# Softmax over a 32,768-wide vocabulary: six 32 KB buffers on one DMA queue, and three 64 KB buffers on two

## The chip, the cores and the metric

The kernel runs on one core of a Trainium2 chip. The metric is device time in microseconds (us) of one execution; the kernel before takes 2494.18 us (median of 3 runs, 2492.26 to 2495.42).

## What is computed

A softmax with temperature over the last axis of a float32 array of 16 x 256 x 32,768; the temperature is 1.0.

```python
scaled = logits / temperature
scaled = scaled - scaled.max(axis=-1, keepdims=True)
exp_scaled = np.exp(scaled)
return (exp_scaled / exp_scaled.sum(axis=-1, keepdims=True)).astype(np.float32)
```

536.87 MB are read and as many are written.

## The kernel before

The 4,096 rows are cut into 8,192 half rows of 16,384 numbers (64 KB). A group is 128 half rows, one on each SBUF partition (64 rows in all), so there are G = 64 groups of 8.4 MB. A group is worked on as C = 2 chunks of 8,192 columns (32 KB on each partition, 4.2 MB), and a chunk has one of six buffers (`xs`, the pool of line 47). There are 128 chunks.

`load` (line 58) brings one chunk in as one DMA; in the first and the last group it uses two DMAs of half the size. `exps` (line 94) does for each piece of 8,192 columns (4,096 in the last group) a maximum on VectorE (line 107, stored negated in `nm`) and, in place, an exponential on ScalarE (line 114) which also adds up its results into `ssum`. `factors` (line 123) finds the maximum of the whole row from the pieces: a small reduction, then `combine` (line 81), which swaps neighbouring partitions, since the two halves of a row lie on neighbouring partitions; a tiny exponential `ee` on ScalarE (line 131), the weighted sum on VectorE (line 138), `combine` again, a reciprocal and the factor `f` of each piece (lines 148 to 150). `scales` (line 152) multiplies a piece by its factor: the first half of the columns on VectorE (line 160), the second half on ScalarE (line 163). `store` (line 70) writes a chunk out as one DMA, in the last group as two.

All loads and stores are issued by SyncE (lines 64 and 75), so they stand in one DMA queue, in the order that the list `order` (line 170) gives: six loads, two stores, and then a load and a store by turns. `keep_in_program_order` holds them to it; a load into a buffer waits for the store that frees it. The order of the instructions of VectorE and ScalarE is chosen by the scheduler of the language: in the trace VectorE takes the next chunk's maximum (line 107) while ScalarE is still at the exponential of the chunk before.

```python
order = [("L", i) for i in range(min(_BUFS, n_chunks))] + [("S", 0)]
for i in range(1, n_chunks):
    order.append(("S", i))
    if i + _BUFS - 1 < n_chunks:
        order.append(("L", i + _BUFS - 1))
```

Of the kernel before, what the change touches and what calls it, by code (L numbers as in the profile page):

```python
# [6 lines left out]


_SPLIT = 2
_CW = 8192  # L10
_BUFS = 6
_PIECE = 8192
_LAST_DMA = 4096
_DVE_SHARE = 0.5


@with_exitstack
def kernel(
    ctx: ExitStack,
    tc: tile.TileContext,  # L20
    logits: bass.AP,
    temperature: bass.AP,
    out: bass.AP,
):
    nc = tc.nc
    inv_t = 1.0 / float(temperature)
    P = nc.NUM_PARTITIONS
    fp32 = mybir.dt.float32
    Exp = mybir.ActivationFunctionType.Exp
    Copy = mybir.ActivationFunctionType.Copy  # L30
    X = mybir.AxisListType.X
    A = mybir.AluOpType

    xf = logits.flatten_outer_dims()
    of = out.flatten_outer_dims()
    N, V = xf.shape
    W = V // _SPLIT
    CW = min(_CW, W)
    C = W // CW
    assert W * _SPLIT == V and CW * C == W and (N * _SPLIT) % P == 0  # L40
    x = xf.rearrange("n (h v) -> (n h) v", h=_SPLIT)
    o = of.rearrange("n (h v) -> (n h) v", h=_SPLIT)
    G = N * _SPLIT // P
    n_chunks = G * C
    n_rounds = _SPLIT.bit_length() - 1

    xpool = ctx.enter_context(tc.tile_pool(name="x", bufs=_BUFS))
    spool = ctx.enter_context(tc.tile_pool(name="stats", bufs=3))
    slots = {}
    stats = {}  # L50

    def spans(total: int, step: int) -> list[tuple[int, int]]:
        return [(s, min(step, total - s)) for s in range(0, total, step)]

    def piece(g: int) -> int:
        return _PIECE if g < G - 1 else min(_PIECE, _LAST_DMA)

    def load(i: int) -> None:
        g, c = divmod(i, C)
        xs = xpool.tile([P, CW], fp32, tag="x", name="xs")  # L60
        slots[i] = xs
        for s, n in spans(CW, _LAST_DMA if g in (0, G - 1) else CW):
            tc.keep_in_program_order(
                nc.sync.dma_start(  # L64
                    out=xs[:, s : s + n],
                    in_=x[g * P : (g + 1) * P, c * CW + s : c * CW + s + n],
                )
            )

    def store(i: int) -> None:  # L70
        g, c = divmod(i, C)
        xs = slots.pop(i)
        for s, n in spans(CW, _LAST_DMA if g == G - 1 else CW):
            tc.keep_in_program_order(
                nc.sync.dma_start(  # L75
                    out=o[g * P : (g + 1) * P, c * CW + s : c * CW + s + n],
                    in_=xs[:, s : s + n],
                )
            )

    def combine(v, op) -> None:
        for j in range(n_rounds):
            mask = [i ^ (1 << j) for i in range(32)]
            nc.vector.stream_shuffle(  # L84
                out=v[:, j + 1 : j + 2], in_=v[:, j : j + 1], mask=mask
            )
            nc.vector.tensor_tensor(  # L87
                out=v[:, j + 1 : j + 2],
                in0=v[:, j : j + 1],
                in1=v[:, j + 1 : j + 2],  # L90
                op=op,
            )

    def exps(i: int) -> None:
        g, c = divmod(i, C)
        xs = slots[i]
        ps = spans(CW, piece(g))
        K = C * len(ps)
        if c == 0:
            stats[g] = tuple(  # L100
                spool.tile([P, K], fp32, tag=f"{nm}{K}", name=nm)
                for nm in ("nm", "ssum", "ee", "f", "ttj")
            )
        nm, ssum = stats[g][:2]
        for j, (s, n) in enumerate(ps):
            k = c * len(ps) + j
            nc.vector.tensor_reduce(  # L107
                out=nm[:, k : k + 1], in_=xs[:, s : s + n], axis=X, op=A.max, negate=True
            )
            if inv_t != 1.0:  # L110
                nc.vector.tensor_scalar_mul(
                    out=nm[:, k : k + 1], in0=nm[:, k : k + 1], scalar1=inv_t
                )
            nc.scalar.activation(  # L114
                out=xs[:, s : s + n],
                in_=xs[:, s : s + n],
                func=Exp,
                bias=nm[:, k : k + 1],
                scale=inv_t,
                accum_out=ssum[:, k : k + 1],  # L120
            )

    def factors(g: int) -> None:
        nm, ssum, ee, f, ttj = stats[g]
        nMh = spool.tile([P, 1 + n_rounds], fp32, tag="nMh", name="nMh")
        Sh = spool.tile([P, 1 + n_rounds], fp32, tag="Sh", name="Sh")
        rS = spool.tile([P, 1], fp32, tag="rS", name="rS")
        with tc.high_priority():
            nc.vector.tensor_reduce(out=nMh[:, 0:1], in_=nm, axis=X, op=A.min)  # L129
            combine(nMh, A.min)  # L130
            nc.scalar.activation(  # L131
                out=ee,
                in_=nm,
                func=Exp,
                bias=nMh[:, n_rounds : n_rounds + 1],
                scale=-1.0,
            )
            nc.vector.tensor_tensor_reduce(  # L138
                out=ttj,
                in0=ee,  # L140
                in1=ssum,
                scale=1.0,
                scalar=0.0,
                op0=A.mult,
                op1=A.add,
                accum_out=Sh[:, 0:1],
            )
            combine(Sh, A.add)
            nc.vector.reciprocal(out=rS, in_=Sh[:, n_rounds : n_rounds + 1])  # L149
            nc.vector.tensor_scalar_mul(out=f, in0=ee, scalar1=rS)  # L150

    def scales(i: int) -> None:
        g, c = divmod(i, C)
        xs = slots[i]
        f = stats[g][3]
        ps = spans(CW, piece(g))
        for j, (s, n) in enumerate(ps):
            k = c * len(ps) + j
            cut = int(n * _DVE_SHARE) // 512 * 512
            nc.vector.tensor_scalar_mul(  # L160
                out=xs[:, s : s + cut], in0=xs[:, s : s + cut], scalar1=f[:, k : k + 1]
            )
            nc.scalar.activation(  # L163
                out=xs[:, s + cut : s + n],
                in_=xs[:, s + cut : s + n],
                func=Copy,
                scale=f[:, k : k + 1],
            )

    order = [("L", i) for i in range(min(_BUFS, n_chunks))] + [("S", 0)]  # L170
    for i in range(1, n_chunks):
        order.append(("S", i))
        if i + _BUFS - 1 < n_chunks:
            order.append(("L", i + _BUFS - 1))

    nxt = 0
    done = -1
    loaded = 0
    for kind, i in order:
        if kind == "L":  # L180
            load(i)
            loaded = i + 1
        else:
            g = i // C
            if g > done:
                while nxt < (g + 1) * C:
                    assert nxt < loaded
                    exps(nxt)
                    nxt += 1
                factors(g)  # L190
                done = g
            scales(i)
            store(i)


# [33 lines left out]
```

## Time and profile before

| What | Value |
|---|---|
| Time, median of 3 runs | 2494.18 us |
| Span of the profiled execution | 2493.8 us |
| VectorE (DVE) busy | 1487.4 us |
| ScalarE (ACT) busy | 1405.0 us |
| Mean DMA rate over the span | 431 GB/s |
| Maximum of 128x8192, L107 (VectorE) | 8.68 us each |
| Exponential of 128x8192, L114 (ScalarE) | 7.12 us each |
| Multiplication of 128x4096, L160 (VectorE) / L163 (ScalarE) | 2.35 / 3.70 us each |

The span is counted from the first to the last instruction of the profiled execution. Busy time of an engine counts its compute instructions only; the issuing of DMAs by SyncE (SP) is not among them. A DMA's transfer is done by 16 DMA engines at once: each of them moves its share of the partitions as a row of packets, one packet for each partition's contiguous run of bytes, and then a small packet that signals the semaphore.

### The profile page before, as it was taken

How to read it: one execution, taken by the hardware profiler on the slowest of the kernel's cores; microseconds unless marked ns; L12 is line 12 of the kernel's file. 1: busy time of each engine (PE TensorE's matmuls, PEld its weight loads, DVE VectorE, ACT ScalarE, POOL GpSimd, SP SyncE). 2: the span in 40 equal slices, each digit the busy share in tenths (PEclk: the TensorE clock that was granted, in tenths of full speed). 3: DMA queues.
4: the chain of work that ended last, by engine and by line, in shares of the span. 5: the costliest groups of instructions: out<-in, count | busy, mean ns of one | idle time of the engine just before them, and what ended most of it. 6: DMA issues, size and time to landing. Idle time of an engine off the chain costs nothing.

```text
span 2493.8 us, 2234 instructions
## 1 busy us (share of the span) xinstructions
DVE 1487.4 (60%) x964; ACT 1405.0 (56%) x455; POOL 0.2 (0%) x4
## 2 busy tenths in 40 slices
DVE  7655565556655566555665566655666566655663
ACT  5665554655556555565555655555546555465553
POOL 0000000000000000000000000000000000000000
DMA  9999999999999999999999999999999999999998
GB/s 412 433 430 432 429 431 432 433 433 434 433 434 432 435 432 435 432 435 431 436 431 435 432 434 433 434 433 433 433 433 433 433 433 434 434 433 434 432 431 368
DMA packets 37745, 1073.90 MB, mean 431 GB/s; under 512 B 4192, under 2 KB 4192, under 8 KB 4192
## 3 DMA queue, kind: packets, MB, share of 16 engines
q1 hardware_dynamic: 37728, 1073.76, 99.9%
q14 instruction: 17, 0.14, 0.0%
HBM read 536.87 MB, written 536.87 MB: 431 GB/s over the span
## 4 chain that ended last, share of the span: by engine, by line
DMA 96%; SPq 1%; ACT 1%; DVE 1%; issue 1%; ACTq 0%
DMA out_dram<-xs 93%; DMA xs<-in_logits_dram 2%; SPq L64 1%; DVE nm L107 1%; ACT xs L163 1%; ACT xs L114 0%; ACTq L224 0%; SPq L75 0%; DVE f L150 0%; ACT ee L131 0%; DVE rS L149 0%; DVE Sh L87 0%; DVE ttj L138 0%; DVE Sh L84 0%; DVE Sh L138 0%
## 5 line engine op out<-in xcount | busy, mean ns | idle before, releaser
L114 ACT ACTIVATE xs<-xs,nm 128x8192 f32<-128x8192 f32 (+1 forms) x130 | 912.1, 7016 | 972.4 <-DVE nm L107 972.4
L107 DVE TENSOR_REDUCE nm<-xs 128x1 f32<-128x8192 f32 (+1 forms) x130 | 1111.6, 8551 | 527.3 <-DMA xs<-in_logits_dram 527.3
L163 ACT ACTIVATE xs<-xs,f 128x4096 f32<-128x4096 f32 (+1 forms) x130 | 468.1, 3648 | 71.4 <-DVE f L150 71.4
L160 DVE TENSOR_SCALAR xs<-xs,f 128x4096 f32<-128x4096 f32 (+1 forms) x130 | 295.7, 2318 | 3.7 <-DVE f L150 1.8
L138 DVE CUSTOM_DVE_ANT_0 ttj<-ee,ssum 128x2 f32<-128x2 f32 x64 | 10.3, 161 | 423.8 <-ACT ee L131 423.8
L114 ACT ACTIVATION_READ_ACCUMULATOR xs<-xs,nm 128x1 f32 x130 | 24.2, 186 | 0.0
L131 ACT ACTIVATE ee<-nm,nMh 128x2 f32<-128x2 f32 x64 | 17.9, 280 | 0.0
L150 DVE TENSOR_SCALAR f<-ee,rS 128x2 f32<-128x2 f32 x64 | 14.6, 229 | 2.2
L149 DVE RECIPROCAL rS<-Sh 128x1 f32<-128x1 f32 x64 | 10.5, 164 | 2.2
L87 DVE TENSOR_TENSOR nMh<-nMh 128x1 f32<-128x1 f32 x64 | 10.2, 160 | 2.2
L87 DVE TENSOR_TENSOR Sh<-Sh 128x1 f32<-128x1 f32 x64 | 10.2, 160 | 2.2
L129 DVE TENSOR_REDUCE nMh<-nm 128x1 f32<-128x2 f32 x64 | 9.9, 155 | 2.2
L84 DVE STREAM_SHUFFLE nMh<-nMh 128x1 f32<-128x1 f32 x64 | 9.7, 151 | 0.0
L84 DVE STREAM_SHUFFLE Sh<-Sh 128x1 f32<-128x1 f32 x64 | 9.7, 151 | 0.0
L114 ACT ACT_TABLE_LOAD x1 | 1.3, 1283 | 12.9 <-DMA xs<-in_logits_dram 12.9
L138 DVE DVE_READ_ACCUMULATOR2_ANT Sh<- 128x1 f32 x64 | 5.3, 84 | 0.0
L84 DVE LOAD_MASK_SELECT Sh<-Sh x64 | 0.9, 14 | 2.8
L84 DVE LOAD_MASK_SELECT nMh<-nMh x64 | 0.9, 14 | 2.7
L210 POOL MEMSET const-bfloat16-1.0<- 128x1 bf16 x1 | 0.1, 102 | 0.0
L210 POOL MEMSET const-uint8-127<- 128x1 uint8 x1 | 0.1, 102 | 0.0
L210 POOL MEMSET const-float32-0.0<- 128x1 f32 x1 | 0.1, 99 | 0.2 <-issue 0.2
L210 POOL MEMSET const-float32-1.0<- 128x1 f32 x1 | 0.1, 99 | 0.0
## 6 DMA issues: line engine op xcount, KB each, us to landing
out_dram<-xs SPq DMA_DIRECT2D x126, 4096.0 KB, 38.2
xs<-in_logits_dram SPq DMA_DIRECT2D x124, 4096.0 KB, 29.0
xs<-in_logits_dram SPq DMA_DIRECT2D x8, 2048.0 KB, 22.3
out_dram<-xs SPq DMA_DIRECT2D x4, 2048.0 KB, 26.7
```

Source lines behind the costliest of these rows:

```text
L64: nc.sync.dma_start(out=xs[:, s : s + n], in_=x[g * P : (g + 1) * P, c * CW + s : c * CW + s + n],)
L84: nc.vector.stream_shuffle(out=v[:, j + 1 : j + 2], in_=v[:, j : j + 1], mask=mask)
L87: nc.vector.tensor_tensor(out=v[:, j + 1 : j + 2], in0=v[:, j : j + 1], in1=v[:, j + 1 : j + 2], op=op,)
L107: nc.vector.tensor_reduce(out=nm[:, k : k + 1], in_=xs[:, s : s + n], axis=X, op=A.max, negate=True)
L114: nc.scalar.activation(out=xs[:, s : s + n], in_=xs[:, s : s + n], func=Exp, bias=nm[:, k : k + 1], scale=inv_t, accum_out=ssum[:, k : k + 1],
L129: nc.vector.tensor_reduce(out=nMh[:, 0:1], in_=nm, axis=X, op=A.min)
L131: nc.scalar.activation(out=ee, in_=nm, func=Exp, bias=nMh[:, n_rounds : n_rounds + 1], scale=-1.0,)
L138: nc.vector.tensor_tensor_reduce(out=ttj, in0=ee, in1=ssum, scale=1.0, scalar=0.0, op0=A.mult, op1=A.add, accum_out=Sh[:, 0:1],)
L149: nc.vector.reciprocal(out=rS, in_=Sh[:, n_rounds : n_rounds + 1])
L150: nc.vector.tensor_scalar_mul(out=f, in0=ee, scalar1=rS)
L160: nc.vector.tensor_scalar_mul(out=xs[:, s : s + cut], in0=xs[:, s : s + cut], scalar1=f[:, k : k + 1])
L163: nc.scalar.activation(out=xs[:, s + cut : s + n], in_=xs[:, s + cut : s + n], func=Copy, scale=f[:, k : k + 1],)
```

## The change

The work is cut differently. A tile is now a whole group (64 KB on each partition), and there are three such buffers instead of six of half the size, at fixed addresses. A load is still made of transfers of 32 KB per partition, two for a tile (four of 16 KB for the first and the last tile). A store is one transfer of 64 KB per partition, and ScalarE issues it on its own DMA queue; the last two tiles' stores are issued by SyncE, the last one in four parts. Maximum and exponential work on pieces of 4,096 columns, four for a tile. The whole multiplication is VectorE's, four pieces of 4,096 columns; ScalarE does none. The program order is fixed by hand: for each tile its maxima and exponentials, the factors, the multiplications, the store, and then the load of the third tile after it. VectorE does not begin a tile's maxima before it is done with the multiplications of the tile before.

The diff, cut to its core:

```diff
--- before.py
+++ after.py
 _SPLIT = 2
-_CW = 8192
-_BUFS = 6
-_PIECE = 8192
-_LAST_DMA = 4096
-_DVE_SHARE = 0.5
+_BUFS = 3
+_LOAD = 8192
+_PIECE = 4096
...
-    xpool = ctx.enter_context(tc.tile_pool(name="x", bufs=_BUFS))
-    spool = ctx.enter_context(tc.tile_pool(name="stats", bufs=3))
-    slots = {}
-    stats = {}
+    pool = ctx.enter_context(tc.tile_pool(name="fixed", bufs=1))
+    bufs = [pool.tile([P, W], fp32, name=f"x{b}") for b in range(_BUFS)]
+    stats = [
+        (
+            [pool.tile([P, K], fp32, name=f"{nm}{b}") for nm in ("nm", "ssum", "ee", "f", "tt")],
+            pool.tile([P, R + 1], fp32, name=f"mx{b}"),
+            pool.tile([P, R + 1], fp32, name=f"su{b}"),
+            pool.tile([P, 1], fp32, name=f"rs{b}"),
+        )
+        for b in range(3)
+    ]
...
     def load(i: int) -> None:
-        g, c = divmod(i, C)
-        xs = xpool.tile([P, CW], fp32, tag="x", name="xs")
-        slots[i] = xs
-        for s, n in spans(CW, _LAST_DMA if g in (0, G - 1) else CW):
-            tc.keep_in_program_order(
-                nc.sync.dma_start(
-                    out=xs[:, s : s + n],
-                    in_=x[g * P : (g + 1) * P, c * CW + s : c * CW + s + n],
-                )
+        step = _PIECE if i in (0, G - 1) else _LOAD
+        for s in range(0, W, step):
+            nc.sync.dma_start(
+                out=bufs[i % _BUFS][:, s : s + step], in_=x[rows(i), s : s + step]
             )
 
     def store(i: int) -> None:
-        g, c = divmod(i, C)
-        xs = slots.pop(i)
-        for s, n in spans(CW, _LAST_DMA if g == G - 1 else CW):
-            tc.keep_in_program_order(
-                nc.sync.dma_start(
-                    out=o[g * P : (g + 1) * P, c * CW + s : c * CW + s + n],
-                    in_=xs[:, s : s + n],
-                )
+        eng = nc.scalar if i < G - 2 else nc.sync
+        step = _PIECE if i == G - 1 else W
+        for s in range(0, W, step):
+            eng.dma_start(
+                out=o[rows(i), s : s + step], in_=bufs[i % _BUFS][:, s : s + step]
             )
...
     def exps(i: int) -> None:
...
+        xs = bufs[i % _BUFS]
+        nm, ssum = stats[i % 3][0][:2]
+        for k in range(K):
+            at = slice(k * _PIECE, (k + 1) * _PIECE)
             nc.vector.tensor_reduce(
-                out=nm[:, k : k + 1], in_=xs[:, s : s + n], axis=X, op=A.max, negate=True
+                out=nm[:, k : k + 1], in_=xs[:, at], axis=X, op=A.max, negate=True
             )
...
             nc.scalar.activation(
-                out=xs[:, s : s + n],
-                in_=xs[:, s : s + n],
+                out=xs[:, at],
+                in_=xs[:, at],
                 func=Exp,
...
-    def factors(g: int) -> None:
...
-        with tc.high_priority():
-            nc.vector.tensor_reduce(out=nMh[:, 0:1], in_=nm, axis=X, op=A.min)
...
     def scales(i: int) -> None:
...
+        xs = bufs[i % _BUFS]
+        (nm, ssum, ee, f, tt), mx, su, rs = stats[i % 3]
+        nc.vector.tensor_reduce(out=mx[:, 0:1], in_=nm, axis=X, op=A.min)
+        combine(mx, A.min)
+        nc.scalar.activation(
+            out=ee, in_=nm, func=Exp, bias=mx[:, R : R + 1], scale=-1.0
+        )
+        nc.vector.tensor_tensor_reduce(
...
+        combine(su, A.add)
+        nc.vector.reciprocal(out=rs, in_=su[:, R : R + 1])
+        nc.vector.tensor_scalar_mul(out=f, in0=ee, scalar1=rs)
+        for k in range(K):
+            at = slice(k * _PIECE, (k + 1) * _PIECE)
             nc.vector.tensor_scalar_mul(
-                out=xs[:, s : s + cut], in0=xs[:, s : s + cut], scalar1=f[:, k : k + 1]
-            )
-            nc.scalar.activation(
-                out=xs[:, s + cut : s + n],
-                in_=xs[:, s + cut : s + n],
-                func=Copy,
-                scale=f[:, k : k + 1],
+                out=xs[:, at], in0=xs[:, at], scalar1=f[:, k : k + 1]
             )
 
-    order = [("L", i) for i in range(min(_BUFS, n_chunks))] + [("S", 0)]
-    for i in range(1, n_chunks):
-        order.append(("S", i))
-        if i + _BUFS - 1 < n_chunks:
-            order.append(("L", i + _BUFS - 1))
...
+    with tc.manual_schedule():
+        for i in range(_BUFS):
             load(i)
...
+        for i in range(G):
+            exps(i)
             scales(i)
             store(i)
+            if i + _BUFS < G:
+                load(i + _BUFS)
```

More of the change, by code (lines that the diff above doesn't have):

```diff
@@ L29 @@
     Exp = mybir.ActivationFunctionType.Exp
-    Copy = mybir.ActivationFunctionType.Copy
     X = mybir.AxisListType.X
@@ L37 @@
     W = V // _SPLIT
-    CW = min(_CW, W)
-    C = W // CW
-    assert W * _SPLIT == V and CW * C == W and (N * _SPLIT) % P == 0
+    K = W // _PIECE
+    assert W * _SPLIT == V and K * _PIECE == W and (N * _SPLIT) % P == 0
     x = xf.rearrange("n (h v) -> (n h) v", h=_SPLIT)
@@ L43 @@
     G = N * _SPLIT // P
-    n_chunks = G * C
-    n_rounds = _SPLIT.bit_length() - 1
-    xpool = ctx.enter_context(tc.tile_pool(name="x", bufs=_BUFS))
-    spool = ctx.enter_context(tc.tile_pool(name="stats", bufs=3))
-    slots = {}
-    stats = {}
[L52 to L56, printed above, removed]
-    def load(i: int) -> None:
-        g, c = divmod(i, C)
-        xs = xpool.tile([P, CW], fp32, tag="x", name="xs")
-        slots[i] = xs
-        for s, n in spans(CW, _LAST_DMA if g in (0, G - 1) else CW):
-            tc.keep_in_program_order(
-                nc.sync.dma_start(
-                    out=xs[:, s : s + n],
-                    in_=x[g * P : (g + 1) * P, c * CW + s : c * CW + s + n],
-                )
+    R = _SPLIT.bit_length() - 1
@@ new lines, with rows @@
+    pool = ctx.enter_context(tc.tile_pool(name="fixed", bufs=1))
[9 more added lines that the diff above has]
+    ]
+    def rows(i: int):
+        return slice(i * P, (i + 1) * P)
@@ L79, in store @@
             )
     def combine(v, op) -> None:
-        for j in range(n_rounds):
-            mask = [i ^ (1 << j) for i in range(32)]
+        for j in range(R):
+            mask = [k ^ (1 << j) for k in range(32)]
             nc.vector.stream_shuffle(
@@ L94, in exps @@
     def exps(i: int) -> None:
[L95 to L102, printed above, removed]
-            )
-        nm, ssum = stats[g][:2]
-        for j, (s, n) in enumerate(ps):
-            k = c * len(ps) + j
+        xs = bufs[i % _BUFS]
+        nm, ssum = stats[i % 3][0][:2]
+        for k in range(K):
+            at = slice(k * _PIECE, (k + 1) * _PIECE)
             nc.vector.tensor_reduce(
-                out=nm[:, k : k + 1], in_=xs[:, s : s + n], axis=X, op=A.max, negate=True
+                out=nm[:, k : k + 1], in_=xs[:, at], axis=X, op=A.max, negate=True
             )
@@ L121, in exps @@
             )
-    def factors(g: int) -> None:
[L124 to L127, printed above, removed]
-        with tc.high_priority():
-            nc.vector.tensor_reduce(out=nMh[:, 0:1], in_=nm, axis=X, op=A.min)
-            combine(nMh, A.min)
-            nc.scalar.activation(
[L132 to L136, printed above, removed]
-            )
[L138 to L160, printed above, removed]
-                out=xs[:, s : s + cut], in0=xs[:, s : s + cut], scalar1=f[:, k : k + 1]
-            )
-            nc.scalar.activation(
-                out=xs[:, s + cut : s + n],
-                in_=xs[:, s + cut : s + n],
-                func=Copy,
-                scale=f[:, k : k + 1],
-            )
@@ L170, with scales @@
-    order = [("L", i) for i in range(min(_BUFS, n_chunks))] + [("S", 0)]
-    for i in range(1, n_chunks):
-        order.append(("S", i))
-        if i + _BUFS - 1 < n_chunks:
-            order.append(("L", i + _BUFS - 1))
[L176 to L180, printed above, removed]
-            load(i)
[L182 to L191, printed above, removed]
+    def scales(i: int) -> None:
+        xs = bufs[i % _BUFS]
[6 more added lines that the diff above has]
+        nc.vector.tensor_tensor_reduce(
+            out=tt,
+            in0=ee,
+            in1=ssum,
+            scale=1.0,
+            scalar=0.0,
+            op0=A.mult,
+            op1=A.add,
+            accum_out=su[:, 0:1],
+        )
+        combine(su, A.add)
[3 more added lines that the diff above has]
+            at = slice(k * _PIECE, (k + 1) * _PIECE)
+            nc.vector.tensor_scalar_mul(
+                out=xs[:, at], in0=xs[:, at], scalar1=f[:, k : k + 1]
+            )
```

## The prediction

> **What bounds the kernel now.** I read the page's engine and DMA rows first. Neither VectorE nor ScalarE is full, and the DMA engines are, in every slice:
>
> ```profile
> span 2493.8 us, 2234 instructions
> DVE 1487.4 (60%) x964; ACT 1405.0 (56%) x455; POOL 0.2 (0%) x4
> ...
> DMA  9999999999999999999999999999999999999998
> ...
> q1 hardware_dynamic: 37728, 1073.76, 99.9%
> ...
> DMA 96%; SPq 1%; ACT 1%; DVE 1%; issue 1%; ACTq 0%
> ```
>
> The packets of the one queue take 99.9% of 16 engines' time, and the chain of work that ended last is DMA for 96%. The waits of SyncE's queue say the same: a load stands ready and waits for the store that frees its buffer.
>
> ```profile
> SPq L64 <- DMA out_dram<-xs: 2246.9, 122, 19.6
> ```
>
> Then I read stretches of the end (us, busy time of the engines, clock, DMA share, GB/s):
>
> ```profile
> 2460.00:2480.00 20.00, 0.00 (x0) 1.75 (x1) 0.00 (x0) 1.00 0.99 426
> 2480.00:2485.00 5.00, 0.00 (x0) 0.00 (x0) 0.00 (x0) 1.00 0.69 295
> 2485.00:2490.00 5.00, 0.00 (x0) 0.00 (x0) 0.00 (x0) 1.00 0.18 79
> 2490.00:2493.80 3.80, 0.00 (x0) 0.00 (x0) 0.00 (x0) 1.00 0.04 17
> ```
>
> Up to 2480 every DMA engine works. Then they drop out one by one: 0.31 x 5 + 0.82 x 5 + 0.96 x 3.8 = 9.3 us of mean idleness, in which a straggler finishes alone. The packet records of the trace say it too: the quickest engines end at 2482.1, the last at 2492.6, and the program 1.25 us later. So the time is four terms: about 1.75 us until the first packet, 2480 us of packets, and 10.4 us for the straggler, and 1.25 us at the end. The profiled span (2493.8) and the median (2494.18) differ by 0.4 us, so I take the sum against the span and add nothing.
>
> **The change part by part.**
>
> *Bytes and packets.* The bytes stay. What a packet costs beyond its bytes comes from two stretches. From 2000 to 2400 us the queue had 5,949 packets, 661 of them small, and 100.3% of 6,400 us: 6,419 / 5,288 = 1.214 us for 32 KB. From 2484 to 2490 us 35 packets of 16 KB took 22.4% of 96 us: 0.614 us. The packet records have 1,213 and 611 ns: 2 x 611 - 1,213 = 9 ns of fixed cost. No 64 KB packet is in the trace; by this line it takes 2 x 1,213 - 9 = 2,417 ns. 63 tiles are stored so, with 8 packets on each engine: 504 pairs x 9 ns = 4.5 us less; as consecutive packets overlap by about 4 ns in the records, only 504 x 5 = 2.5 us. With 63 fewer transfers (262 become 132 + 67 = 199) 63 semaphore packets of 9 ns go too: 0.6 us. I take **-4 us**; the bounds are -5.1 and 0 (a 64 KB row could travel as two packets). The first loads and last stores keep their 16 KB packets.
>
> *Two queues.* Loads and stores no longer stand in one row. The queue before reached 433 GB/s from 2000 to 2400 us with a DMA share of 1.00, so there is no idle share for a second queue to fill; value taken: 0. No row has two queues at work, so the bounds are wide: on the good side, the straggler's 10.4 us; on the bad side, the disturbance described under the rivals, +40 us.
>
> The Trainium skill (DMA: Bandwidth & Descriptors, "Issuing engines are not separate DMA queues") speaks against a gain here: transfers issued from several engines share the same 16 DMA engines and interleave, so only the issuing time is saved. By it the term is 0 as well. The same page ("Where 436 GB/s comes from") has a ceiling of 435 GB/s; an estimate from that page is 1073.74 MB / 435.2 = 2467 us for the bytes alone, and no run here shows more than the 433.
>
> *ScalarE issues the stores.* A DMA issue is 0.38 us (L75), and the waiting store blocks what is behind it on ScalarE: the next tile's exponentials. These wait for a maximum that VectorE begins only after the same multiplications, and that takes 4.41 us (128x4096). So the issue is covered, at no cost; without that cover it would be 64 x 0.4 = 26 us spread over tiles that have slack.
>
> *The computing, now a serial chain.* All multiplications go to VectorE and nothing of the next tile is done beside them. Rows for the length:
>
> ```profile
> L107 DVE TENSOR_REDUCE nm<-xs 128x1 f32<-128x4096 f32 x4 | 17.6, 4414 | 3.9 <-DMA xs<-in_logits_dram 3.9
> L160 DVE TENSOR_SCALAR xs<-xs,f 128x4096 f32<-128x4096 f32 x126 | 290.8, 2350 | 3.7 <-DVE f L150 1.8
> ...
> 2448.93 3.71 ACT L114 ACTIVATE xs<-xs,nm 128x4096 f32<-128x4096 f32 x1 [1.07 <-DVE nm L107]
> ...
> 2454.01 4.87 DVE L160 TENSOR_SCALAR xs<-xs,f 128x2048 f32<-128x2048 f32 x4
> ```
>
> Four maxima are 17.7 us. From the last exponential's start to the first multiplication the timeline has 2454.01 - 2448.93 = 5.1 us, the factors included. Four multiplications are 9.4 us. Together **32.2 us** a tile, against 2493.8 / 64 = 38.97 us that the DMA engines need for its two transfers. VectorE rises to about 64 x 28.4 = 1,820 us busy, ScalarE falls to 64 x 15.9 = 1,020 us, and 6.8 us a tile are left over: cost 0, as long as the DMA engines have something to move meanwhile.
>
> *Three buffers.* A buffer goes through load, computing and store, and must be round in 3 x 38.97 = 116.9 us. Alone a transfer takes 38.97 / 2 = 19.5 us, shared with the other direction throughout 39. Each also needs its hand-over: the first issue is at 0.73 and the first packet at 1.75 us (1.0), and the first maximum starts at 12.89, though 16 packets of 0.61 from 1.75 us end at 11.5 (1.4). Even with both transfers shared throughout it is 39 + 32.2 + 39 + 2 x 2.4 = 115 us. That fits, by 2 us at worst and by 41 us with transfers alone. The DMA engines go idle only when all three buffers are in computing or hand-over together; the sum takes 0 for it.
>
> *The end.* Before, the last load lands at 2444.5 us while stores for 35 us more are queued: nothing of the last computing shows. After, two things are behind the last load: the store of tile 62 (19.5 us) and tile 63. Let R be what is left to move of load 63 when the multiplications of tile 62 end. Tile 63's first stored piece is ready 17.7 + 5.1 + 2.35 + 1.1 = 26.2 us later, if its data are there, and the DMA engines have R + 19.5 us until then. R = 0 leaves 6.7 us idle, R = 6.8 none. With a larger R the last piece is late: it lands at about 2R, and is stored 1.4 + 4.4 + 5.1 + 2.35 + 1.1 = 14.4 us later; R = 9.7 costs 19.4 + 14.4 - 29.2 = 4.6 us, R = 19.5 14.4 us. In a regular rhythm VectorE waits 6.8 us a tile for a load, so R near 6.8 to 10 is what I expect: **+2 us** (0 to 14.4).
>
> **Sum:** 2493.8 - 4 + 2 + 0 = 2491.8, so **2491.5 us**.
>
> **Rivals.**
>
> *The straggler goes (faster).* Packet records show why some engines are late: in the first 500 us the last packets of a load that stands ahead of stores stretch from 1.21 to as much as 2.4 us, on some engines and not on others; later they hardly do. With two queues each engine reads and writes all the time, and such turns from all reading to all writing may not occur. Up to 10.4 us less: 2481 to 2487. Against it: some of the late engines also lose 0.7 us at a time, some 20 times in all over the whole run, which the change does not obviously touch.
>
> *The same disturbance becomes permanent (slower).* The stretch after the first stores has it at its plainest:
>
> ```profile
> 45.00:60.00 15.00, 14.89 (x7) 15.00 (x5) 0.00 (x0) 1.00 1.04 426
> 60.00:65.00 5.00, 4.89 (x7) 3.36 (x4) 0.00 (x0) 1.00 0.83 347
> ```
>
> The rate falls to 347 GB/s where all engines turn from loads to stores at once. Between 65 and 400 us the worst engines lose about 1.9 us in each 100 us, until the engines have drifted apart. After the change a load starts on all 16 engines at the same moment, when a store has landed on all of them; that could hold them in step for good: 24.9 x 1.9 = 47, less some 7 that are in the time before: +40, half of it if half the turns suffer. 2505 to 2532 us. It decides if steady stretches show under 430 GB/s.
>
> *The end is exposed (slower).* R at 0, or near a whole load, instead of near 7 us: +7 to +14 on the sum without an end term, 2497 to 2504. It decides if the DMA share falls between the last load and the last store.
>
> *It does not do what it says.* 64 KB rows as two packets: 2493 to 2495, inside the forecast's own range.
>
> **How the numbers follow.** The forecast, own range 2486 to 2497: 0.55. Straggler gone: 0.15. End exposed: 0.18. Permanent disturbance: 0.12. The range 2483 to 2508 leaves out about 0.06 below and 0.1 above. A measurement of this kernel can tell about 0.2% (5 us: 2489.2 to 2499.2) from no change. Faster: 0.15 + a quarter of 0.55 = 0.29. Slower: 0.12 + 0.13 of the exposed end = 0.25. The same: 0.46.
>
> **What would show it.** Right: DMA share 0.99 to 1.00 in every slice but the last; about 2,417 ns per 64 KB packet (the queue of ScalarE: some 8,064 data packets, half of what the stores had); VectorE near 1,820 us; VectorE's maxima waiting for loads, some 6.8 us a tile. Wrong: slices with a share of 0.97 or less in the middle (buffers too few, or disturbance), a gap between the last load and the last store, or engines that all end together.

## The result: 5.8% slower, and the profile after

| | Before | After |
|---|---|---|
| Time, median of 4 runs each | 2493.56 us | 2638.9 us (2624.82 to 2657.32) |
| Ratio after / before, 95% interval | | 1.0584 (1.0546 to 1.0621) |
| Time of the profiled execution / its span | 2494.18 / 2493.8 us | 2624.82 / 2623.0 us |
| DMA engines: durations of their packets (mean of 16) | 2490.8 us | 2553.8 us |
| the remainder of the span (idle) | 3.0 us | 69.2 us |

The forecast was 2491.5 us in a range of 2483 to 2508: the sign is wrong, and the time lies 131 us above the range. The page of after, its first rows: busy time of the engines, the DMA share by slices and the queues.

```profile
span 2623.0 us, 2542 instructions
DVE 1783.3 (68%) x1216; ACT 986.3 (38%) x577; POOL 0.2 (0%) x4
...
DMA  9999998999899999999999999999999999899996
GB/s 416 422 417 419 421 433 373 436 421 424 358 431 429 408 386 398 425 410 420 414 397 412 402 378 423 403 428 421 413 408 422 414 414 415 366 421 438 421 416 299
...
q1 hardware_dynamic: 19728, 553.66, 50.1%
q10 hardware_dynamic: 8928, 520.10, 47.3%
```

VectorE and ScalarE did what was worked out for them (1,820 and 1,020 us were forecast). The DMA row has a 9 in nearly every slice, as before, and yet the rate beneath it is 409 GB/s in the mean, against 431. A 9 stands for 90% or more, so this row alone would mislead; the rate doesn't. The two queues together hold 97.4%, and before one queue held 99.9%.

So the 129.2 us by which the span grew come in two kinds. From the packet records: each packet has a duration that it has most of the time (611, 1,213 and 2,418 ns for 16, 32 and 64 KB), and what it takes above that I call **stretch**. It is 3.8 us for each DMA engine before and 71.4 after. Hence 63.0 us more of packets, although the same packets at their usual durations would have cost some 4 us less, and 66.2 us more idle. (Consecutive packets overlap by some 4 ns, which the sum of durations counts twice: 5 to 8 us a run, by which this "idle" is too small in every kernel, before's as well. The records don't name the engine of a packet. I sorted them onto 16 engines by which ends where the next begins; sums over all engines don't depend on that, readings of one engine do.)

The steady stretch from 1000 to 1400 us shows the first kind. DMA rows of after, and of a kernel from below (`half_stores`), over the same 400 us:

```profile
DMA packets 4237, 163.53 MB, mean 409 GB/s; under 512 B 476, under 2 KB 476, under 8 KB 476
...
q1 hardware_dynamic: 2844, 82.84, 49.6%
q10 hardware_dynamic: 1391, 80.68, 49.3%
```

```profile
DMA packets 5954, 173.14 MB, mean 433 GB/s; under 512 B 668, under 2 KB 668, under 8 KB 668
...
q1 hardware_dynamic: 2976, 86.61, 50.2%
q10 hardware_dynamic: 2975, 86.51, 50.1%
```

The engines are occupied for 98.9% of the time in after, and move 163.5 MB where 173.1 are possible: most of the loss here is in the duration of packets, not in gaps.

The second kind is in some dozen places. Stretches of after around one of them: VectorE, ScalarE and GpSimd busy, clock, DMA share, GB/s.

```profile
660.00:670.00 10.00, 10.00 (x3) 6.02 (x3) 0.00 (x0) 1.00 0.99 416
670.00:679.00 9.00, 6.80 (x6) 7.95 (x5) 0.00 (x0) 1.00 0.94 408
679.00:692.00 13.00, 11.36 (x12) 1.42 (x3) 0.00 (x0) 1.00 0.34 146
692.00:700.00 8.00, 8.00 (x3) 4.40 (x3) 0.00 (x0) 1.00 0.89 332
```

For 13 us only a third of the DMA engines' time is used. The timeline gives the frame (start, duration, engine):

```profile
659.06 0.34 ACTq L68 DMA_DIRECT2D out_dram<-x  x1
...
681.51 9.14 DVE L129 TENSOR_SCALAR x<-x,f 128x4096 f32<-128x4096 f32 x4
...
690.68 0.34 ACTq L68 DMA_DIRECT2D out_dram<-x  x1
693.09 1.60 SPq L60 DMA_DIRECT2D x<-in_logits_dram  x2
```

A store is issued at 659.06. SyncE issues the load into its buffer only at 693.09, since the whole store has to land first. Why that lasts is in the packet records of two DMA engines (S a 64 KB store packet, L a 32 KB load packet, start in us + duration in ns):

```
a prompt one:  ... L658.2+1222 L659.5+1218 S660.7+3366 S664.0+2418 S666.5+2418 S668.9+2418
               S671.3+2418 S673.7+2418 S676.1+2418 S678.5+2418  (idle until 691.6)
the last one:  ... L661.3+2373 L663.8+1211 S665.0+2418 L667.4+1213 S668.6+2418 S671.0+2418
               L673.4+1213 S674.6+2418 L677.0+1213 S678.2+2418 L680.7+1213 S681.9+2418
               L684.3+1213 S685.5+2418 L687.9+1213 S689.1+2418 L691.5+1213 L692.7+1213
```

The prompt engine has no loads left and sends its eight store packets in a row. The last one still has loads, and serves **one packet of each queue in turn**: a load packet goes before nearly every store packet, and the store is done only at 691.5. Of three buffers one is being stored, one computed, and one has its data nearly everywhere: there is nothing to move for the engines that are through. The waits of SyncE's queue say it as a sum, and the issues say how long each transfer is on its way (us to landing):

```profile
SPq L60 <- DMA out_dram<-x: 2440.9, 61, 68.1
```

```profile
x<-in_logits_dram SPq DMA_DIRECT2D x124, 4096.0 KB, 47.5
...
out_dram<-x ACTq DMA_DIRECT2D x62, 35.1
```

Turns are by packet, not by byte. While both queues have work, the store with its 64 KB packets gets two thirds of the time.

### The profile page after: what moved, and what is told of

Same layout as the page of the kernel before. It is cut to its first block, busy times and chain, and to the rows that moved or that the text cites. A ratio compares the mean times of both kernels' runs of the same rounds, so it can differ in the third digit from the quotient of the medians.

```text
span 2623.0 us, 2542 instructions
## 1 busy us (share of the span) xinstructions
DVE 1783.3 (68%) x1216; ACT 986.3 (38%) x577; POOL 0.2 (0%) x4
## 5 line engine op out<-in xcount | busy, mean ns | idle before, releaser
L97 ACT ACTIVATE x<-x,nm 128x4096 f32<-128x4096 f32 x256 | 949.2, 3708 | 1602.5 <-DVE nm L90 1564.6
L90 DVE TENSOR_REDUCE nm<-x 128x1 f32<-128x4096 f32 x256 | 1116.5, 4412 | 578.7 <-DMA x<-in_logits_dram 578.7
L129 DVE TENSOR_SCALAR x<-x,f 128x4096 f32<-128x4096 f32 x256 | 585.0, 2349 | 2.6 <-DVE f L126 0.4
L114 DVE CUSTOM_DVE_ANT_0 tt<-ee,ssum 128x4 f32<-128x4 f32 x64 | 10.5, 164 | 226.1 <-ACT ee L111 226.1
L97 ACT ACTIVATION_READ_ACCUMULATOR x<-x,nm 128x1 f32 x256 | 47.7, 186 | 0.0
L111 ACT ACTIVATE ee<-nm,mx 128x4 f32<-128x4 f32 x64 | 18.0, 282 | 0.0
L126 DVE TENSOR_SCALAR f<-ee,rs 128x4 f32<-128x4 f32 x64 | 14.7, 229 | 2.2
L125 DVE RECIPROCAL rs<-su 128x1 f32<-128x1 f32 x64 | 10.5, 164 | 2.2
L78 DVE TENSOR_TENSOR su<-su 128x1 f32<-128x1 f32 x64 | 10.2, 160 | 2.2
L78 DVE TENSOR_TENSOR mx<-mx 128x1 f32<-128x1 f32 x64 | 10.2, 159 | 2.2
## 6 DMA issues: line engine op xcount, KB each, us to landing
x<-in_logits_dram SPq DMA_DIRECT2D x124, 4096.0 KB, 47.5
out_dram<-x ACTq DMA_DIRECT2D x62, 35.1
```

Source lines behind the costliest of these rows:

```text
L78: nc.vector.tensor_tensor(out=v[:, j + 1 : j + 2], in0=v[:, j : j + 1], in1=v[:, j + 1 : j + 2], op=op,)
L90: nc.vector.tensor_reduce(out=nm[:, k : k + 1], in_=xs[:, at], axis=X, op=A.max, negate=True)
L97: nc.scalar.activation(out=xs[:, at], in_=xs[:, at], func=Exp, bias=nm[:, k : k + 1], scale=inv_t, accum_out=ssum[:, k : k + 1],)
L111: nc.scalar.activation(out=ee, in_=nm, func=Exp, bias=mx[:, R : R + 1], scale=-1.0)
L114: nc.vector.tensor_tensor_reduce(out=tt, in0=ee, in1=ssum, scale=1.0, scalar=0.0, op0=A.mult, op1=A.add, accum_out=su[:, 0:1],)
L125: nc.vector.reciprocal(out=rs, in_=su[:, R : R + 1])
```

## The experiments

The names in capitals are those of the recorded expectations. All edits are to after, unless something else is said, and all ratios are to before, measured on the same chip. "Stretch" and "idle" are per DMA engine, in the profiled execution, as above. That is one of the runs, and for kernels whose runs differ it isn't the median: 2624.8 us for after, 2534.7 for `full_loads`, 2552.3 for `row_order_loads`, 2617.1 for `free_two_queues`.

### One queue again, everything else kept

```diff
# one_queue
-        eng = nc.scalar if i < G - 2 else nc.sync
+        eng = nc.sync
...
-            if i + _BUFS < G:
-                load(i + _BUFS)
+            if i >= 1 and i + 2 < G:
+                load(i + 2)
```

> The kernel after, with all stores on SyncE's queue too and each load issued one store later (store 1, load 3, store 2, load 4, ...), so that a load waits for a store that is one transfer back. Three theories of the 130 us. IN STEP: with two queues, whenever a queue runs empty and starts again, all 16 engines turn between reading and writing at the same moment, and such a turn stretches packets by about 0.3 us; the idle time follows from engines that were stretched more than others. BUFFERS: three whole-tile buffers are too few; the engines have nothing to move while one of them still finishes a store. MIXING: reads and writes taken in turn from two queues slow each other, in step or not. IN STEP and MIXING expect 2482 to 2495 us (one queue that never empties). BUFFERS expects over 2550 us, since the three buffers are the same.

Measured: 2496.12 us (2495.40 to 2496.34), ratio 1.0006 (0.9997 to 1.0015). That is 1 us above what IN STEP and MIXING expected; BUFFERS, with over 2550 us, falls as the whole cause. Stretch 4.5 us, idle 7.6. The page's first row and its queue:

```profile
span 2494.5 us, 2540 instructions
...
q1 hardware_dynamic: 28656, 1073.75, 99.7%
```

The three buffers, the serial chain of computing and the 64 KB packets stay as in after and cost nothing together: 143 us of the loss need the second queue, with the order that goes with it.

### The same order on one queue

The order was changed in that run too. Here it isn't: only the store's queue is.

```diff
# stores_on_sync
-        eng = nc.scalar if i < G - 2 else nc.sync
+        eng = nc.sync
```

> The kernel after with its stores on SyncE's queue and nothing else changed: the load of the third tile after stands right behind its own buffer's store in the one queue and waits for it there, so that store and load never overlap. It tells what the second queue is worth in this order of the program. ONE QUEUE IS FINE expects the engines to lose only the hand-over from store to load, about 2.4 us a tile: 2620 to 2660 us. If the wait also delays the next store, more: up to 2900 us. No stretch in either case.

Measured: 2723.05 us (2722.8 to 2723.39), ratio 1.0917 (1.09 to 1.0933): above the first range and inside the second, but not for the reason given there. Idle 121 us (a gap of some 1.9 us for each tile, in which the queue waits for a store before the load behind it can be issued) and stretch 118, where I had expected none: all engines are restarted together, and their load packets 0, 6 and 7 of a transfer take 272, 242 and 415 ns more than usual in the mean. So in the order of after the second queue is worth 84 us; in the order of `one_queue`, which has a load issued behind the store of another buffer, none is needed.

### The second queue alone, on the kernel before

```diff
# before_two_queues (edit of before)
-                nc.sync.dma_start(
+                nc.scalar.dma_start(
                     out=o[g * P : (g + 1) * P, c * CW + s : c * CW + s + n],
```

> The kernel before, with its stores issued by ScalarE on its own queue and nothing else changed (six buffers, 32 KB transfers both ways). MIXING expects the stretch of the kernel after, 60 us or more: 2550 us and up. BUFFERS expects 2490 to 2500 us, since there are six buffers. IN STEP expects something between, 2510 to 2600 us: loads wait for stores on the other queue, so a queue can run empty and start again on all engines at once.

Measured: 2926.17 us (2925.57 to 2929.14), ratio 1.1733 (1.1715 to 1.175). Stretch 83 us and over 2550 us are what MIXING expected, but the greater part is idle time, 354 us, which none of the three had. The waits tell of another cause than the one that I wanted to see (engine, what waits and for what, us in total, times, longest):

```profile
ACT xs L163 <- DVE f L150: 1046.5, 62, 17.6
```

In this kernel ScalarE also multiplies. With the stores in its stream, each waiting there for its multiplications, its work on the next tile comes late, and VectorE's factors with it: so I read this row (71.4 us in all before), without a run that tries the order by itself. Of the queues this run tells one thing: 32 KB packets on both don't prevent stretch. That 72 of its 83 us of stretch lie on the packets around a queue's restart was a hint, which the next ones follow.

### Half the store transfer

```diff
# half_stores
-        step = _PIECE if i == G - 1 else W
+        step = _PIECE if i == G - 1 else _LOAD
```

> The kernel after, with each store in two transfers of 32 KB per partition instead of one of 64 KB, so that half a buffer comes free earlier. BUFFERS expects most of the 66 us of idle DMA time to go: 2550 to 2585 us. IN STEP expects as many turns or more, and the idle time to follow the stretch: 2600 to 2660 us. MIXING expects no change in the stretch, and 2600 us or more.

Measured: 2493.22 us (2493.07 to 2493.57), ratio 0.9995 (0.9986 to 1.0004). All expectations missed (BUFFERS had only the idle time right), and the whole loss is gone: stretch 2.7 us, idle 1.7. The page:

```profile
span 2491.4 us, 2664 instructions
...
DMA  9999999999999999999999999999999999999998
...
q1 hardware_dynamic: 19872, 553.66, 51.6%
q10 hardware_dynamic: 17856, 520.10, 48.4%
...
x<-in_logits_dram SPq DMA_DIRECT2D x124, 4096.0 KB, 41.1
out_dram<-x ACTq DMA_DIRECT2D x124, 4096.0 KB, 38.0
```

So a second queue alone isn't to blame: it is here. (Here a load is issued while its queue still has some 13 to 20 us of packets left on each engine; none starts on all engines at once.) The one thing left is the store as one transfer of 64 KB per partition beside loads of 32. It does three things at once: larger packets, one completion instead of two for a buffer, and queues that run through the partitions at different speeds.

### Halves, but late

Two transfers could also help by releasing half a buffer earlier. Here the right half goes first and both after the last multiplication.

```diff
# half_stores_late
-        step = _PIECE if i == G - 1 else W
-        for s in range(0, W, step):
+        step = _PIECE if i == G - 1 else _LOAD
+        for s in reversed(range(0, W, step)) if step == _LOAD else range(0, W, step):
```

> The kernel with half stores (2493 us), with the two halves of a tile's store issued the other way about: the right half first, both when all of the tile is multiplied. Packets, transfers and queues are the same, but the left half, which the next load wants first, now comes free last, so that the load queue can run empty before it starts again. EARLY RELEASE (what saved the half stores is that the load queue never runs empty beside a running store) expects the stretch of the 64 KB against 64 KB run to come back, some 0.8 us a tile: 2520 to 2560 us. EQUAL PACKETS (it is enough that both queues have the same packets) expects 2490 to 2502 us.

Measured: 2493.38 us (2492.91 to 2493.91), ratio 0.9995 (0.9986 to 1.0005), stretch 2.7, idle 1.8. The first half's store no longer starts before the tile is complete, and the time is the same. At first a load is still issued some 4 to 5 us before its queue would run empty. This lead shrinks, and from about 1950 us on the load queue does run empty on most engines, beside a running store. The queues from 2291 to 2296 us:

```profile
q10 hardware_dynamic: 61, 1.97, 91.0%
q1 hardware_dynamic: 6, 0.20, 9.1%
```

All the same the 250 us from 2000 on have only 0.09 us of stretch. So EARLY RELEASE falls: the half stores need neither the earlier start nor a load queue that never empties. EQUAL PACKETS had this time; that equal packets are enough everywhere is refuted by `before_two_queues` above and by two kernels below.

### One transfer, small packets

Sixteen floats of padding between the halves of a buffer's row make two 32 KB packets of each partition's row, in one transfer with one completion.

```diff
# one_store_small_packets
-    bufs = [pool.tile([P, W], fp32, name=f"x{b}") for b in range(_BUFS)]
+    bufs = [pool.tile([P, 2, W // 2 + _PAD], fp32, name=f"x{b}") for b in range(_BUFS)]
...
+        if step == W:
             eng.dma_start(
-                out=o[rows(i), s : s + step], in_=bufs[i % _BUFS][:, s : s + step]
+                out=o[rows(i), :].rearrange("p (h v) -> p h v", h=2),
+                in_=bufs[i % _BUFS][:, :, : W // 2],
             )
```

> The kernel after, with the same one store of 64 KB per partition, but made of two packets of 32 KB for each partition: a gap of 64 bytes lies between the halves of each buffer, so a partition's run of bytes ends there. Buffers, waits and the number of transfers are those of the kernel after. The halved stores took the whole loss away, and they changed two things, packets and the moment at which half a buffer comes free. PACKETS (64 KB packets on one queue beside 32 KB packets on the other are what stretches, and the idle time follows from it) expects 2485 to 2505 us. BUFFERS (a whole buffer must be through on all engines before its load starts) expects the idle 66 us to stay: 2550 us or more. IN STEP (all engines turn together) expects 2600 us or more.

Measured: 2563.12 us (2561.25 to 2573.34), ratio 1.0283 (1.0258 to 1.0308). Idle falls from 69 to 15.5 us, stretch only from 71.4 to 60.5: neither PACKETS nor BUFFERS has it alone. Most of the idle time goes with the size of the packets, the stretch does not. The issues fit the former: with equal packets, a store of 8 MB and a load, which waits for the other of its pair, take about as long.

```profile
x<-in_logits_dram SPq DMA_DIRECT2D x124, 4096.0 KB, 41.9
out_dram<-x ACTq DMA_DIRECT2D x62, 8192.0 KB, 43.0
```

### Loads as large as the stores

```diff
# full_loads
-_LOAD = 8192
+_LOAD = 16384
```

> The kernel after, with each load in one transfer of 64 KB per partition too (first and last tile as they are). In the packet records of the kernel after a store's packet is stretched by 700 ns where the load's packet before it on the same DMA engine has the same place in its transfer (the same partition), by some 50 ns elsewhere. KEEPING PACE (loads and stores of one tile must have the same number of packets in the same order; then the two queues, served in turn, stay a fixed distance apart and never meet) expects little stretch and 2488 to 2515 us. BUFFERS (whole buffers come free too late) expects idle time to stay: 2550 us or more. LARGE STORES (64 KB stores beside another queue are bad whatever the loads) expects 2560 us or more.

Measured: 2523.39 us (2515.62 to 2534.68), ratio 1.0104 (1.0081 to 1.0127). Idle 3.6 us: with equal packets the idle time is gone, although buffers and completions are as in after (BUFFERS falls). The time is above KEEPING PACE's range and below that of LARGE STORES, so all three missed. Stretch 51 us, 47 of it at restarts: the load queue runs empty once a tile; the first packet of the store that begins then takes 533 ns more in the mean (33 of the 51 us), the first packet of the load that comes back 171 (11 us). With the padding, and the loads in one transfer in the same row order, the time is similar:

```diff
# row_order_loads (edit of one_store_small_packets)
+        if step == _LOAD:
+            nc.sync.dma_start(
+                out=bufs[i % _BUFS][:, :, : W // 2],
+                in_=x[rows(i), :].rearrange("p (h v) -> p h v", h=2),
+            )
+            return
```

> The kernel with one store of two 32 KB packets for each partition (2563 us), with each load made the same way: one transfer, both halves of a partition one after the other. The store is not touched. KEEPING PACE expects the 60 us of stretch to go, 2488 to 2510 us, though a load now lands whole. BUFFERS expects no gain, 2560 us or more.

Measured: 2531.16 us (2515.4 to 2552.25), ratio 1.0125 (1.005 to 1.0199), between the two expectations; stretch 36, idle 29. So equal packets don't always end the idle time. It is of another kind here: gaps of 1 to 3 us, one about every 120 us, where those of after last up to 13 us. No run isolates their cause.

### The transfers alone

Six kernels leave out all computation. SyncE loads into two buffers, ScalarE stores a buffer of zeros, and nothing waits for anything but its own queue and buffer. They differ in the packet sizes of load and store; the sixth, at the end, in where it stores.

```diff
# free_two_queues (32 KB loads, 64 KB stores; the core of the kernel)
+        nc.vector.memset(const, 0.0)
+        for i in range(G):
+            load(i)
+            store(i)
# free_32_32 and free_load64_store32: the store in two transfers; the latter, and free_64_64:
-_LOAD = 8192
+_LOAD = 16384
# free_load16_store32: the store in two transfers, and
-_LOAD = 8192
+_LOAD = 4096
```

> Transfers alone: this kernel leaves out all of the computation. SyncE loads the 64 tiles in 32 KB transfers into two buffers that nobody reads; ScalarE stores one constant buffer 64 times in 64 KB transfers; neither queue waits for the other and none runs empty. MIXING expects the packets stretched all the way, and 2530 us or more. IN STEP expects stretch only until the engines have drifted apart, and under 2500 us. BUFFERS expects about 2485 us, with no stretch.

> Transfers alone, as in the run with two free queues, with the stores of the constant buffer in 32 KB packets as the loads. All computation is left out. PACKETS expects no stretch and about 2485 to 2500 us. IN STEP expects the same stretch as with 64 KB stores, about 110 us on each engine: 2570 us or more.

> Transfers alone, loads and stores both in 64 KB packets, all computation left out. If PACKETS is about unequal sizes: no stretch, 2485 to 2500 us. If it is about 64 KB packets on two queues: stretch as before or more, 2570 us or more.

> Transfers alone, loads in 64 KB packets and stores in 32 KB packets, all computation left out: the sizes of the kernel after changed about. Unequal sizes expects stretch of the same order, 2550 to 2620 us. If 64 KB stores alone are to blame: no stretch, 2485 to 2500 us.

> Transfers alone, all computation left out: loads in packets of 16 KB, stores in packets of 32 KB, so again two load packets for each store packet but no 64 KB packet. KEEPING PACE expects stretch of the order of the 64 and 32 KB run (112 us on each engine), 2540 to 2640 us. LARGE STORES expects none, 2484 to 2495 us.

| Load / store packets | Time, us (range) | Ratio, 95% | Stretch, us |
|---|---|---|---|
| 32 / 64 KB | 2602.52 (2582.07 to 2617.1) | 1.0405 (1.0353 to 1.0458) | 112 |
| 32 / 32 KB | 2486.61 (2486.55 to 2486.73) | 0.9965 (0.9952 to 0.9979) | 2.1 |
| 64 / 64 KB | 2509.68 (2506.45 to 2512.92) | 1.0059 (1.0039 to 1.0079) | 6.2 |
| 64 / 32 KB | 2486.01 (2485.34 to 2486.24) | 0.9964 (0.9949 to 0.998) | 3.6 |
| 16 / 32 KB | 2547.37 (2544.82 to 2549.92) | 1.0211 (1.0189 to 1.0233) | 53.5 |

The 64 / 64 and 16 / 32 KB rows have two runs each. The first row makes the stretch without any computing, and is MIXING's number. The second, which takes reads and writes in turn just as well, makes none, so MIXING falls; its queues, then those of 16 / 32 KB:

```profile
DMA packets 36866, 1073.77 MB, mean 432 GB/s; under 512 B 4096, under 2 KB 4096, under 8 KB 4096
...
q1 hardware_dynamic: 18432, 536.88, 50.1%
q10 hardware_dynamic: 18432, 536.88, 50.0%
```

```profile
DMA packets 55300, 1073.80 MB, mean 421 GB/s; under 512 B 6144, under 2 KB 6144, under 8 KB 6144
...
q1 hardware_dynamic: 36864, 536.89, 50.8%
q10 hardware_dynamic: 18432, 536.88, 49.3%
```

In the 32 / 32 kernel all engines alternate in step, all 16 of them on the same queue for 54% of the time from 250 to 1250 us (36% of the whole), and lose nothing by it: IN STEP, which goes back to a rival of the prediction, falls. Unequal sizes alone aren't it either (64 / 32 loses nothing, a miss), nor do the packets have to be of 64 KB (16 / 32 has 53.5 us of stretch: LARGE STORES falls; KEEPING PACE had this time, with twice this stretch). The 64 / 64 kernel loses its 23 us at the end, where engines are done between 2476 and 2504 us; why is not known.

What the two bad rows have in common: the store's packets are twice as large as the load's, so with turns by packet the stores are through first (the issues have 38.6 and 19.4 us to landing for a store, 81.8 and 55.1 for a load), and each next one starts beside a load queue that is somewhere in the middle. That this is what stretches the packets is argued from the two rows, not shown. In 32 / 64 a store packet that follows a load packet of the same place among an engine's eight of a transfer, 0 to 7 (that is, of the same partition), is the slow one. Mean excess over 2,418 ns, in after: 399, 728, 711, 726, 731, 359 ns at places 1 to 6, and mostly 0 to 100 at other pairs of places. To see whether the row's address in HBM or the partition makes the meeting, the stores were written one row further on (the first output row stays unwritten):

```diff
# free_store_shifted (edit of free_two_queues)
-            nc.scalar.dma_start(out=o[rows(i), s : s + W], in_=const[:, s : s + W])
+            nc.scalar.dma_start(out=o[i * P + (i < G - 1) : (i + 1) * P + (i < G - 1), s : s + W], in_=const[:, s : s + W])
```

> Transfers alone, all computation left out: the run with 64 KB stores and 32 KB loads (2602 us), with each store written one row (64 KB) further on in memory (but for the last tile); the partition that it is read from stays. If a store and a load collide because they use the same partition of the on-chip memory, the 700 ns stay where both are at the same place of their transfers. If they collide by their addresses in HBM (the same row of a tile, tiles being 8 MB apart), the stretched pairs move by one: a store at place 1 with a load at place 2. The time should stay within 2560 to 2640 us either way.

Measured: 2601.63 us (2599.6 to 2603.67), ratio 1.0428 (two runs). The slow pairs stay where they were: 351, 688, 731, 833, 893 ns at the equal places 1 to 5, less at the others. Shifting the HBM row by one doesn't matter; what they share is the partition, or only the place in the transfer, which no run separates. The meeting explains only part of the stretch.

## Why the prediction was wrong

**What held.** The bound: the time is still that of the DMA engines. *Bytes and packets*: a 64 KB row is one packet, 2,418 ns for 2,417 forecast; without stretch the packets of `one_queue` take 2486.9 - 4.5 = 2482.4 us and those of before 2490.8 - 3.8 = 2487.0, so 4.6 us less for the 4 that I took. *ScalarE issues the stores*: no ScalarE wait for it matters in after, and in `half_stores` twice as many issues cost nothing. Uncovered it would not have been 26 us: in `before_two_queues`, whose ScalarE has other tiles' work behind its stores, the same move ends 431 us later, as I read its waits. *The computing*: 1783 and 986 us busy, and the serial chain fits, since `one_queue` and `half_stores` have it and take 2496 and 2493 us. *Three buffers*: enough, for both of these have three. *The end*: with the DMA shares of `half_stores` from 2460 us on (0.88 of 15, 0.95 of 10, 0.09 of 6.4 us) it leaves 8.1 us idle, for the 9.3 before; there +2 was about 0. (The sum itself gives 2491.8; the 0.3 us to 2491.5 have no reason, and don't matter.)

**The step that failed** is *Two queues*, "value taken: 0". Its reason was that the one queue had no idle share for a second to fill: true, but it speaks only against a gain. The bound on the bad side was +40, which the range up to 2508 didn't even take in; the term measured 71.4 - 3.8 = 67.6 us of stretch in after, and brought 66 us of idle time with it that no bound held. The size of the second is a false assumption in *Three buffers*: "shared with the other direction throughout 39" supposes that load and store share by halves. They share by packets, the store's being twice as large, so a load of half the bytes takes 47.5 us to land (the second of a pair waits for the first) and a store 35.1; and an engine that lags sends a load packet before each store packet, while the others have nothing to do. `full_loads` and `one_store_small_packets` show it: equal packets, same buffers, idle 3.6 and 15.5.

The Trainium skill's rule that was weighed there (DMA: Bandwidth & Descriptors, "Issuing engines are not separate DMA queues": transfers of several engines interleave on the same 16, and only issuing time is saved) agrees with `free_32_32`, where the second queue brings nothing to the rate: 432 GB/s against 433. It speaks of what can be saved; that the interleaving can cost 145 us is in the runs, and the runs decide. The same page ("Queues, rings and completion order") says that an engine takes turns between queues by packets, and puts typically some 9 to 17 descriptors into a packet. The turns by packets are as it says; in the records here each is of one row, 32 or 64 KB, and where that is less than the page has, the measurement decides.

**The rival** that came nearest, *the same disturbance becomes permanent* (0.12), had the right sign and a fault of the right kind: half of after's stretch (36.6 us of 71.4) is on the two packets at a queue's first turn after a run of the other, and 13.6 us on neighbours of the same partition. Its cause, a load that starts on all 16 engines at the same moment and holds them in step, is not enough: being in step costs nothing in `free_32_32`, nor do such starts late in `half_stores_late`. Its point of decision (rates under 430 GB/s) was right.

*The end is exposed* came about in after, as part of the idle time: two gaps after the last load was issued hold 16 of the 69 us.

```profile
2563.00:2577.00 14.00, 11.35 (x12) 2.43 (x3) 0.00 (x0) 1.00 0.27 116
2595.00:2603.00 8.00, 5.75 (x10) 2.04 (x3) 0.00 (x0) 1.00 0.25 107
```

In the first, most engines have nothing left to move while tile 62 is computed, the prediction's R = 0; whether engines that lag brought it about, as at 680 us, no run tells. *The straggler goes* is so in after (its last 16 packets end between 2621.0 and 2621.7 us), without any gain. *It does not do what it says* did not come about.

**Where it went**, by changes from after (times are medians; stretch and idle are of the profiled execution):

| Kernel | Store packets and transfers | Time, us | Profiled, us | Stretch | Idle |
|---|---|---|---|---|---|
| after | 64 KB, one | 2638.9 | 2624.8 | 71.4 | 69 |
| one_store_small_packets | 32 KB, one | 2563.1 | 2564.3 | 60.5 | 15.5 |
| row_order_loads | 32 KB, one; loads too | 2531.2 | 2552.3 | 36 | 29 |
| full_loads | 64 KB, one; loads too | 2523.4 | 2534.7 | 51 | 3.6 |
| half_stores | 32 KB, two | 2493.2 | 2493.2 | 2.7 | 1.7 |
| one_queue | 64 KB, one; one queue | 2496.1 | 2496.3 | 4.5 | 7.6 |

Shown: the whole loss hangs on one element, the store as one transfer of 64 KB rows on a second queue beside 32 KB loads; the long gaps of its idle half on unequal packets with turns by packet; its other half is stretch. What is **not settled** is why a packet stretches. In after it shows most where a queue gets its turn again after a run of the other, and where neighbours share a partition. But `full_loads` loses 47 us on 244 packets per engine at such turns, and `free_load64_store32`, whose load queue is empty once a tile for some ten store packets, only 2.4 us on 254. (`half_stores` has some 500 and loses 0.8 us on them, but its runs are of two packets, where a completion packet took its queue's turn; no queue is empty there.) Nor do equal packets prevent it: `before_two_queues` has 83 us, `full_loads` 51. Restarts and meetings are where it shows, not yet why. No kernel here that does the whole work beats before by more than can be measured: the interval of the best, `half_stores`, includes 1.

## What to carry to other kernels

"The DMA engines are full, so a second queue changes nothing" leaves out the side that can lose: price it by whether both queues have packets of one size, transfers of one shape, and always another transfer waiting. Kernels with all three, in packets of 32 KB, lost nothing here; which of them is needed alone is not shown, and loads of 64 KB beside stores of 32 lost nothing either. A larger store transfer isn't safe just because its fixed cost is lower: here it saved 4 us and lost 145, and cutting it into the loads' shape gave all of it back. When the busy row reads 9 throughout, read the rate beneath it and the mean duration of a packet before saying that the engines are at their limit.

## What the runs showed of the hardware

- A DMA engine serves two queues one packet from each in turn (records of S and L above, 64 and 32 KB): shares go by packet size. A completion packet of 9 ns takes a turn too.
- A row of 64 KB travels as one packet of 2,418 ns, 8 ns less than two of 32 KB.
- Two queues with equal 32 KB packets, both kept filled, reach 432 GB/s and 2486.6 us for all bytes, in step or not: the bare transfers are only some 9 us below the kernel before on the same chip (2495.2).
- A store packet of 64 KB behind a 32 KB load packet of its own partition took 0.4 to 0.9 us longer in the mean at places 1 to 5 of a transfer, also with the store's HBM row shifted by one (351 to 893 ns in `free_store_shifted`).
- One queue that is emptied and refilled once a tile lost 1.9 us a tile idle and as much again in stretched packets (2723.05 us).
